# Turning rows into channel order: 32x32 blocks on VectorE and a trip through DRAM in place of TensorE transposes

## The chip, the cores and the metric

The kernel runs on one core of a Trainium2 chip. Its engines are TensorE (PE in the profile, its weight loads PEld), VectorE (DVE), ScalarE (ACT), GpSimd (POOL) and SyncE (SP); SyncE and GpSimd here mostly issue DMAs. The metric is the device time of one execution in microseconds, lower is better, given as the median of several runs.

## The reference

One decoder layer on x of 2048 tokens by 1024 channels, float32, batch 1:

```python
h = _rmsnorm(x, norm1_w)
proj = h @ w_in                                   # 1024 -> 3840 columns
hg_p, rw_p = proj[..., :HG_COLS], proj[..., HG_COLS:]
o_hg = _hgrn2_mixer(...)                          # 4 heads of 128, gated linear recurrence, chunks of 64
rw_p = rw_p + (_token_shift(rw_p) - rw_p) * rw_shift_mu
o_rw = _rwkv7_mixer(...)                          # 8 heads of 64, delta-rule state update
x = x + concatenate([o_hg, o_rw], axis=-1) @ w_out
x = x + _conv_ffn(_rmsnorm(x, norm2_w), w_up, conv_w, conv_b, w_down)
return _rmsnorm(x, final_norm_w)

def _rmsnorm(x, w):
    return x * rsqrt(mean(x * x, axis=-1) + 1e-6) * w
```

The norms need a token's whole row in one partition (tokens on partitions, channels along the free axis). The matrix products need the channels on partitions. So each normed block has to be transposed.

## The kernel before

The tokens are cut into NBLK = 4 blocks of BLK = 512. Phase 1 (up to some 1330 us) does the first norm, the input projection, both mixers and the output projection; phase 2 the up projection, the convolution and the down projection. Matrix products run in three terms (mm3: high by high, high by low, low by high), on operands split into two float32r parts.

Phase 1 is written as three streams that are interleaved by hand: dense (line 516), rw_stream (a super-step of two head pairs, rw_super, line 647) and hg_stream (one head, hg_unit, line 942). Each pass of the last loop takes one step of the two recurrent streams and then as much of the dense stream as a credit of TICK = 2000 ns pays for (fill, line 1100); the numbers that dense yields (648 for a projection's three matmuls, 436 for four transposes) are these costs. The framework's scheduler then makes each engine's order from this program; within an engine (and a DMA queue) instructions run strictly in that order.

The dense stream's jobs of a block are one "A" (the block's operand hh, hl gets ready), then 30 "P" (a projection of 128 columns, eight steps of three matmuls into a bank of the pair "pj", emptied by ScalarE and VectorE). From block 2 on, an "O" (the output projection of block nb - 2, out_block, line 379) stands ahead of "A". A list called extra puts further jobs between these, by position from "A":

- load4 (line 420) loads 512 rows into row_tile, the one tile "xt" of 128 x 4 x 1024, as four DMAs of 128 rows; norm4 (line 427) scales each row by its reciprocal root mean square (rstd, line 128, on ScalarE).
- For the next block's x: "E" load at +18, norm at +22, and "T" at +25, which is turn (line 437): for each of the KD = 8 slices of 128 channels, four TensorE transposes into a pj bank, which ScalarE copies back into xt in place. Later split_h (line 447), called during the last job before the next "A", multiplies by norm1_w (per partition) and splits into hh and hl.
- For the second norm of block nb - 2 (blocks 0 and 1): load at +6 of x1d (the sum of x and the output projection, in DRAM), norm at +10, and "N" at +11, which is transposed (line 258) with to_h2 (line 490): four transposes a slice into pj, ScalarE empties the bank with norm2_w as a scale per partition, and SyncE's queue stores the slice to h2d in DRAM, from which phase 2 reads.

The first block's x is transposed in another way, at the start, and blocks 2 and 3 of the second norm in phase 2; neither is touched.

Most DMAs go through SyncE's queue (the function dma). Two of its users matter for the chain: in rw_super, Ed<-M (line 745) stores parts of the masked products M to DRAM and E<-Ed (line 748) loads them back in the layout in which VectorE solves the triangular systems (lines 800 and 802). The ring "wraw" (four buffers of 2 KB per partition) holds raw weights in block 0, raw w_out tiles in "O", and the squares of rstd.

Of the kernel before, what the change touches and what calls it, by code (L numbers as in the profile page):

```python
# [7 lines left out]
F32 = mybir.dt.float32  # L8
# [4 lines left out]
ALU = mybir.AluOpType  # L13
# [54 lines left out]
def tile_layer(ctx, tc, consts, x, norm1_w, w_in, hg_lb_logits, hg_norm_w, rw_shift_mu, rw_w0, rw_w2,  # L68
# [14 lines left out]
    def row_tile():  # L83
        return xp_.tile([P, 4, D], F32, tag="xt", name="xt", bufs=1)
# [29 lines left out]
    def act(out_, in_, func, **kw):  # L114

        want = tables.get(func)
        if want is not None and want != tab["now"]:
            pre = S.preload_act_table_set(want)
            for u_ in tab["uses"]:
                tc.add_manual_dep(pre.ins, u_.ins.name, NOSYNC, reason="table order")  # L120
            tab.update(now=want, pre=pre, uses=[])
        i_ = S.activation(out_, in_, func, **kw)  # L122
        if want is not None:
            tc.add_manual_dep(i_.ins, tab["pre"].ins.name, NOSYNC, reason="table order")
            tab["uses"].append(i_)
        return i_

    def rstd(pool, xt, name, sqt="nsq", sqb=1):

        sq = pool.tile([P, D], BF16, tag=sqt, name="nsq", bufs=sqb)  # L130
        st = pool.tile([P, 2], F32, tag="nst", name=name, bufs=8)
        act(sq, xt, AF.Square, accum_out=st[:, 0:1])
        act(st[:, 1:2], st[:, 0:1], AF.Ln, bias=eps6, scale=1.0 / D)
        act(st[:, 1:2], st[:, 1:2], AF.Exp, scale=-0.5)
        return st[:, 1:2]
# [23 lines left out]
    def vec(nm, i):  # L159
        return vt[:, off[nm] + i:off[nm] + i + 1]  # L160
# [23 lines left out]
    oT = [dp.tile([D, BLK], F32, name=f"oT{b}") for b in range(NBLK)]  # L184
    x1d = [dp.tile([BLK, D], F32, name=f"x1d{b}") for b in range(NBLK)]
    h2d = [dp.tile([D, BLK], F32, name=f"h2d{b}") for b in range(NBLK)]
    gd_ = [dp.tile([FF, BLK], F32, name=f"gd{b}") for b in range(NBLK)]
    KH = NFF // 2
    DS = 5
# [84 lines left out]
    def phase1(c1):  # L274
# [22 lines left out]
        def bank(kind):  # L297
            return ps.tile([P, 512], F32, tag=kind, name=kind, bufs=2)
# [119 lines left out]
        rows = {}  # L418

        def load4(key, src, r0):  # L420
            def f():
                rows[key] = row_tile()
                for i in range(4):
                    dma(rows[key][:, i, :], src[r0 + i * P:r0 + (i + 1) * P, :])
            return f

        def norm4(key):
            def f():
                for i in range(4):
                    t_ = rows[key][:, i, :]  # L430
                    V.tensor_scalar_mul(t_, t_, rstd(wp, t_, "nst", "wraw", 4))
            return f

        def four_tiles(t_):
            return [t_[:, i, :] for i in range(4)]

        def turn(nb):

            t_ = rows[nb]
            for k in range(KD):  # L440
                tp = bank("pj")
                for i in range(4):
                    TE.transpose(tp[:, i * P:(i + 1) * P], t_[:, i, k * P:(k + 1) * P], ident)
                act(t_[:, :, k * P:(k + 1) * P], tp.rearrange("p (i t) -> p i t", i=4), AF.Copy)
                yield 436

        def split_h(nb, k):

            src, w = rows[nb][:, :, k * P:(k + 1) * P], vec("n1", k)
            h4, l4 = (t_[:, k, :].rearrange("p (i t) -> p i t", i=4) for t_ in (hh, hl))  # L450
            act(h4, src, AF.Copy, scale=w)
            V.scalar_tensor_tensor(l4, src, w, h4.bitcast(F32), ALU.mult, ALU.subtract)

        def next_block(nb, k):

# [30 lines left out]
        def to_h(k, tp, w):  # L486
            act(hh[:, k, :], tp, AF.Copy, scale=w)
            V.scalar_tensor_tensor(hl[:, k, :], tp, w, hh[:, k, :].bitcast(F32), ALU.mult, ALU.subtract)  # L488

        def to_h2(nb):  # L490
            def evict(k, tp, w):
                t_ = wp.tile([P, BLK], F32, tag="wraw", name="h2", bufs=4)
                act(t_, tp, AF.Copy, scale=w)
                dma(h2d[nb][k * P:(k + 1) * P, :], t_)
            return evict

        def constants():

# [17 lines left out]
        def dense():  # L516
# [27 lines left out]
            for nb in range(NBLK):  # L544
                if nb + 1 < NBLK:
                    extra += [(at[nb] + 18, ("E", load4(nb + 1, x[0], (nb + 1) * BLK))),
                              (at[nb] + 22, ("E", norm4(nb + 1))), (at[nb] + 25, ("T", nb + 1))]
                if nb >= 2:
                    extra += [(at[nb] + 6, ("E", load4(("N", nb - 2), x1d[nb - 2], 0))),
                              (at[nb] + 10, ("E", norm4(("N", nb - 2)))), (at[nb] + 11, ("N", nb - 2))]  # L550
            for m in range(2):
                extra += [(at[3] + 14 + 5 * m, ("E", sum_load(m))), (at[3] + 17 + 5 * m, ("E", sum_make(m)))]
            extra += [(at[3] + 25 + m, ("W", 2, o_take(m))) for m in range(4)]
# [27 lines left out]
            for n, jb in enumerate(jobs):  # L581
                if jb[0] == "E":
                    jb[1]()
                    continue
                if jb[0] == "A":
                    if jb[1] == 0:
                        banks = spread()
                        ahead = transposed(four_tiles(rows[0]), "n1", lambda: next(banks), to_h)
                    continue
                if jb[0] == "T":  # L590
                    yield from turn(jb[1])
                    continue
                if jb[0] == "N":
                    yield from transposed(four_tiles(rows.pop(jb)), "n2", lambda: bank("pj"), to_h2(jb[1]))
                    continue
                if jb[0] in "OW":
                    while done["rw2"] < 2 * jb[1] + 2 or done["hg"] < 4 * jb[1] + 4:
                        yield None
                    if jb[0] == "W":
                        jb[2]()  # L600
                    else:
                        yield from (out_block(2, *rows["O"]) if jb[1] == 2 else out_block(jb[1], then=jb[1] + 2))
                    continue
                _, col, ev, cond, fin = jb
                while not cond():
                    yield None
                load(i)
                ws = loaded.pop(i)
                if i == 0:
                    next(ahead)  # L610
                    next(ahead)
                    constants()
                load(i + 1)
                i += 1
                acc = bank("pj")
                then = jobs[n + 1][1] if jobs[n + 1][0] == "A" else None
                for k in range(KD):
                    wh, wl = ws[k // 4]
                    next(ahead, None)
                    mm3(acc, (wh[:, k % 4, :], wl[:, k % 4, :]), (hh[:, k, :], hl[:, k, :]), k == 0, k == KD - 1)  # L620
                    if k == KD - 1:
                        ev(acc)
                        if fin is not None:
                            fin()
                    next_block(then, k)
                    yield 648
# [996 lines left out]
```

## Time and profile before

| | us |
|---|---|
| median of 3 runs | 2657.88 |
| lowest and highest | 2653.09, 2657.88 |
| the profiled execution | 2662.58 |
| its span in the trace | 2660.8 |
| PE busy | 2560.2 (96%) |
| DVE busy | 1952.9 (73%) |
| ACT busy | 1389.2 (52%) |
| POOL busy | 380.4 (14%) |

Busy time is the union of an engine's instructions; a matmul's recorded duration overlaps the next one's, since matmuls are pipelined. A row of the groups reads: line, engine, operation, tile written <- tiles read, shapes, count | busy us, mean ns of one | idle us of the engine just before them, and what ended it. Lines are those of the kernel before; in the changed kernel the same code stands 1 to 10 lines lower. PEclk is the granted TensorE clock as a share of full speed.

### The profile page before, as it was taken

The numbers are of one execution on the slowest core, as the hardware profiler recorded it, in microseconds if no ns is written. First come the engines' busy times: TensorE is split into PE (matmuls) and PEld (weight loads), VectorE is DVE, ScalarE is ACT, GpSimd is POOL, SyncE is SP. The second block draws the span as 40 slices with busy tenths as digits, with TensorE's granted clock in tenths as the row PEclk, the third lists the DMA queues.
The fourth block names the chain that finished last, engine by engine and source line by source line (L and its number), as shares of the span: only waits on it lengthen the run. The fifth ranks groups of instructions, "written<-read, shape, count | busy, mean of one in ns | idle before, by whom it ended". The sixth has DMA issues, their size and how long they took to land. (4 is left out here: it accounts for less than half of the span.)

```text
span 2660.8 us, 51050 instructions
## 1 busy us (share of the span) xinstructions
PE 2560.2 (96%) x19595; PEld 2061.2 (77%) x19595; DVE 1952.9 (73%) x3728; ACT 1389.2 (52%) x2274; POOL 380.4 (14%) x686
## 2 busy tenths in 40 slices
PE   7999999989999999999899999999999999999998
PEld 5777777766777777777678888887888887888887
DVE  4877667576567765767678789987998887766556
ACT  5566453545535555445456754456545544545444
POOL 6433222212222122222100000000000000000000
PEclk9999999999999999999999999999999999999999
DMA  8645443445643456744493468646763553998665
GB/s 303 204 165 170 158 143 120 130 148 203 199 143 126 156 196 199 276 131 136 154 309 113 143 204 266 233 154 225 245 203 131 166 189 127 327 320 286 197 191 186
DMA packets 312714, 510.59 MB, mean 192 GB/s; under 512 B 46879, under 2 KB 143509, under 8 KB 312469
## 3 DMA queue, kind: packets, MB, share of 16 engines
q1 hardware_dynamic: 257937, 328.99, 37.4%
q0 software_dynamic: 54464, 178.32, 20.4%
q8 instruction: 154, 2.52, 0.4%
q14 instruction: 91, 0.75, 0.1%
q10 hardware_dynamic: 68, 0.02, 0.0%
HBM read 372.99 MB, written 134.22 MB: 191 GB/s over the span
## 5 line engine op out<-in xcount | busy, mean ns | idle before, releaser
L270 PE MATMUL pj<-hh,wh 128*128 128x512 f32 x960 | 393.4, 410 | 6.2 <-ACT rkv L122 3.3
L271 PE MATMUL pj<-hl,wh 128*128 128x512 f32 x960 | 377.8, 394 | 1.3 <-issue 1.3
L272 PE MATMUL pj<-hh,wl 128*128 128x512 f32 x960 | 377.5, 393 | 0.0
L270 PE MATMUL ua<-Bh,uwh 128*128 128x512 f32 x704 | 276.4, 393 | 4.4 <-ACT m L122 3.1
L272 PE MATMUL ua<-Bh,uwl 128*128 128x512 f32 x704 | 274.6, 390 | 0.0
L271 PE MATMUL ua<-Bl,uwh 128*128 128x512 f32 x704 | 274.3, 390 | 0.0
L270 PEld LDWEIGHTS pj<-hh,wh 128*128 128x128 f32 x960 | 181.5, 189 | 55.2 <-issue 8.7
L272 PEld LDWEIGHTS pj<-hh,wl 128*128 128x128 f32 x960 | 181.1, 189 | 40.6 <-issue 1.7
L271 PEld LDWEIGHTS pj<-hl,wh 128*128 128x128 f32 x960 | 181.6, 189 | 34.3 <-DVE hl L488 0.5
L254 ACT CAST uwh<-uraw 128x512 fp32r<-128x512 f32 x220 | 134.2, 617 | 128.9 <-PE ua L271 55.7
L255 DVE TENSOR_TENSOR dal<-draw,dah 128x512 fp32r<-128x512 f32 x138 | 95.4, 691 | 113.4 <-ACT dah L254 113.2
L255 DVE TENSOR_TENSOR uwl<-uraw,uwh 128x512 fp32r<-128x512 f32 x220 | 147.6, 688 | 34.9 <-ACT uwh L254 34.8
L254 ACT CAST dah<-draw 128x512 fp32r<-128x512 f32 x138 | 85.7, 621 | 164.9 <-PE da L271 80.6
L270 PEld LDWEIGHTS ua<-Bh,uwh 128*128 128x128 f32 x704 | 132.2, 188 | 34.1 <-ACT m L122 5.7
L272 PEld LDWEIGHTS ua<-Bh,uwl 128*128 128x128 f32 x704 | 132.3, 188 | 28.1 <-DVE uwl L255 0.4
L271 PEld LDWEIGHTS ua<-Bl,uwh 128*128 128x128 f32 x704 | 132.3, 188 | 26.7
L270 PE MATMUL ud<-Bh,uwh 128*128 128x512 f32 x352 | 138.1, 392 | 0.0
L272 PE MATMUL ud<-Bh,uwl 128*128 128x512 f32 x352 | 137.2, 390 | 0.0
L271 PE MATMUL ud<-Bl,uwh 128*128 128x512 f32 x352 | 137.1, 390 | 0.0
L1493 POOL DMA_DIRECT2D gd<-y x2 | 1.1, 540 | 946.8 <-DVE y L1491 946.8
L271 PE MATMUL da<-dbl,dah 128*128 128x512 f32 x332 | 129.5, 390 | 0.2 <-DVE dbl L255 0.2
L272 PE MATMUL da<-dbh,dal 128*128 128x512 f32 x332 | 129.3, 389 | 0.0
(584 smaller groups left out, 6233.9 us busy)
## 6 DMA issues: line engine op xcount, KB each, us to landing
uraw<-in_w_up_dram SPq DMA_DIRECT2D x176, 256.0 KB, 3.1
woraw<-in_w_out_dram POOLq DMA_DIRECT2D x96, 256.0 KB, 3.6
br<-gd SPq DMA_DIRECT2D x88, 256.0 KB, 4.2
draw<-Sg SPq DMA_DIRECT2D x88, 256.0 KB, 3.3
draw<-Tw SPq DMA_DIRECT2D x88, 256.0 KB, 4.0
gd<-y SPq DMA_DIRECT2D x86, 256.0 KB, 2.9
Sg<-br SPq DMA_DIRECT2D x72, 256.0 KB, 2.1
xt<-x1d SPq DMA_DIRECT2D x32, 512.0 KB, 6.7
```

The lines of the kernel that those rows point to most:

```text
L254: S.copy(hi, src)
L255: V.tensor_sub(lo, src, hi.bitcast(F32))
L270: TE.matmul(acc, lh, rh, start=first, stop=False, skip_group_check=skip)
L271: TE.matmul(acc, lh, rl, start=False, stop=False, skip_group_check=skip)
L272: TE.matmul(acc, ll, rh, start=False, stop=last, skip_group_check=skip)
L1493: (dma if end is None else nc.gpsimd.dma_start)(gd_[2 * h + b][fb * P:(fb + 1) * P, :], ys[0][:, b * BLK:(b + 1) * BLK])
```

## The change

For the x rows of blocks 1, 2 and 3 and the second norm of blocks 0 and 1, the TensorE transposes go. load4 now puts the 512 rows into xt so that partition group g (32 partitions) holds the 128 tokens g * 128 to g * 128 + 127, as four runs i of 32. turn becomes one VectorE transpose in 32x32 blocks for each slice of 128 channels, from xt into a tile "turned" of the ring wraw, and four stores (one for each partition group, 32 partitions x 4 runs of 512 bytes) that put the blocks in channel order into a DRAM tile: the new hT for x, h2d for the second norm. For x a new function back loads hT into a new xt, eight DMAs of 128 x 512, and split_h reads that. For the second norm the weight norm2_w is broadcast to all partitions (two tiles n2row) and multiplied in norm4, along with the row's scale.

The jobs "T" and "N" go. The eight turns of x stand at +23 to +26, two at each position, and back at +29; of the second norm, the norm stands at +9 and its turns at +10 to +13. The yields of 436 go with the transposes, so the dense stream's other jobs move up against the two recurrent streams, and the scheduler makes all orders anew.

```diff
--- before.py
+++ after.py
@@ -184,6 +184,7 @@
     oT = [dp.tile([D, BLK], F32, name=f"oT{b}") for b in range(NBLK)]
     x1d = [dp.tile([BLK, D], F32, name=f"x1d{b}") for b in range(NBLK)]
     h2d = [dp.tile([D, BLK], F32, name=f"h2d{b}") for b in range(NBLK)]
+    hT = [dp.tile([D, BLK], F32, name=f"hT{b}") for b in range(NBLK)]
     gd_ = [dp.tile([FF, BLK], F32, name=f"gd{b}") for b in range(NBLK)]
     KH = NFF // 2
     DS = 5
@@ -418,38 +419,58 @@
         rows = {}
 
         def load4(key, src, r0):
+
             def f():
                 rows[key] = row_tile()
-                for i in range(4):
-                    dma(rows[key][:, i, :], src[r0 + i * P:r0 + (i + 1) * P, :])
+                v = src[r0:r0 + BLK, :].rearrange("(g i t) d -> g t i d", g=4, i=4)
+                for g in range(4):
+                    dma(rows[key][g * 32:g * 32 + 32], v[g])
             return f
 
         def norm4(key):
             def f():
+                w = None
+                if isinstance(key, tuple):
+                    w = [wp.tile([P, BLK], F32, tag="wraw", name="n2row", bufs=4) for _ in range(2)]
+                    for c in range(2):
+                        dma(w[c], norm2_w[0:1, c * BLK:(c + 1) * BLK].broadcast_to([P, BLK]))
                 for i in range(4):
                     t_ = rows[key][:, i, :]
-                    V.tensor_scalar_mul(t_, t_, rstd(wp, t_, "nst", "wraw", 4))
+                    r_ = rstd(wp, t_, "nst", "wraw", 4)
+                    if w is None:
+                        V.tensor_scalar_mul(t_, t_, r_)
+                        continue
+                    for c in range(2):
+                        h_ = t_[:, c * BLK:(c + 1) * BLK]
+                        V.scalar_tensor_tensor(h_, h_, r_, w[c], ALU.mult, ALU.mult)
             return f
 
         def four_tiles(t_):
             return [t_[:, i, :] for i in range(4)]
 
-        def turn(nb):
-
-            t_ = rows[nb]
-            for k in range(KD):
-                tp = bank("pj")
-                for i in range(4):
-                    TE.transpose(tp[:, i * P:(i + 1) * P], t_[:, i, k * P:(k + 1) * P], ident)
-                act(t_[:, :, k * P:(k + 1) * P], tp.rearrange("p (i t) -> p i t", i=4), AF.Copy)
-                yield 436
+        def turn(key, dst, k):
+
+            def f():
+                y = wp.tile([P, 4, 4, 32], F32, tag="wraw", name="turned", bufs=4)
+                V.transpose(y.rearrange("p c i t -> p i c t"),
+                            rows[key][:, :, k * P:(k + 1) * P].rearrange("p i (c t) -> p i c t", t=32))
+                for g in range(4):
+                    dma(dst[k * P:(k + 1) * P, g * P:(g + 1) * P].rearrange("(c p) x -> p c x", p=32),
+                        y[g * 32:g * 32 + 32].rearrange("p c i t -> p c (i t)"))
+            return f
+
+        def back(nb):
+            def f():
+                t_ = rows[nb] = row_tile().rearrange("p i (a t) -> p (i a) t", t=BLK)
+                for k in range(KD):
+                    dma(t_[:, k, :], hT[nb][k * P:(k + 1) * P, :])
+            return f
 
         def split_h(nb, k):
 
-            src, w = rows[nb][:, :, k * P:(k + 1) * P], vec("n1", k)
-            h4, l4 = (t_[:, k, :].rearrange("p (i t) -> p i t", i=4) for t_ in (hh, hl))
-            act(h4, src, AF.Copy, scale=w)
-            V.scalar_tensor_tensor(l4, src, w, h4.bitcast(F32), ALU.mult, ALU.subtract)
+            src, w = rows[nb][:, k, :], vec("n1", k)
+            act(hh[:, k, :], src, AF.Copy, scale=w)
+            V.scalar_tensor_tensor(hl[:, k, :], src, w, hh[:, k, :].bitcast(F32), ALU.mult, ALU.subtract)
 
         def next_block(nb, k):
 
@@ -486,13 +507,6 @@
         def to_h(k, tp, w):
             act(hh[:, k, :], tp, AF.Copy, scale=w)
             V.scalar_tensor_tensor(hl[:, k, :], tp, w, hh[:, k, :].bitcast(F32), ALU.mult, ALU.subtract)
-
-        def to_h2(nb):
-            def evict(k, tp, w):
-                t_ = wp.tile([P, BLK], F32, tag="wraw", name="h2", bufs=4)
-                act(t_, tp, AF.Copy, scale=w)
-                dma(h2d[nb][k * P:(k + 1) * P, :], t_)
-            return evict
 
         def constants():
 
@@ -544,10 +558,12 @@
             for nb in range(NBLK):
                 if nb + 1 < NBLK:
                     extra += [(at[nb] + 18, ("E", load4(nb + 1, x[0], (nb + 1) * BLK))),
-                              (at[nb] + 22, ("E", norm4(nb + 1))), (at[nb] + 25, ("T", nb + 1))]
+                              (at[nb] + 22, ("E", norm4(nb + 1))), (at[nb] + 29, ("E", back(nb + 1)))]
+                    extra += [(at[nb] + 23 + k // 2, ("E", turn(nb + 1, hT[nb + 1], k))) for k in range(KD)]
                 if nb >= 2:
                     extra += [(at[nb] + 6, ("E", load4(("N", nb - 2), x1d[nb - 2], 0))),
-                              (at[nb] + 10, ("E", norm4(("N", nb - 2)))), (at[nb] + 11, ("N", nb - 2))]
+                              (at[nb] + 9, ("E", norm4(("N", nb - 2))))]
+                    extra += [(at[nb] + 10 + k // 2, ("E", turn(("N", nb - 2), h2d[nb - 2], k))) for k in range(KD)]
             for m in range(2):
                 extra += [(at[3] + 14 + 5 * m, ("E", sum_load(m))), (at[3] + 17 + 5 * m, ("E", sum_make(m)))]
             extra += [(at[3] + 25 + m, ("W", 2, o_take(m))) for m in range(4)]
@@ -586,12 +602,6 @@
                     if jb[1] == 0:
                         banks = spread()
                         ahead = transposed(four_tiles(rows[0]), "n1", lambda: next(banks), to_h)
-                    continue
-                if jb[0] == "T":
-                    yield from turn(jb[1])
-                    continue
-                if jb[0] == "N":
-                    yield from transposed(four_tiles(rows.pop(jb)), "n2", lambda: bank("pj"), to_h2(jb[1]))
                     continue
                 if jb[0] in "OW":
                     while done["rw2"] < 2 * jb[1] + 2 or done["hg"] < 4 * jb[1] + 4:
```

## The prediction

> **What bounds the kernel now.** The page's first part comes first: busy time, share of the span and instructions of each engine.
>
> ```profile
> span 2660.8 us, 51050 instructions
> PE 2560.2 (96%) x19595; PEld 2061.2 (77%) x19595; DVE 1952.9 (73%) x3728; ACT 1389.2 (52%) x2274; POOL 380.4 (14%) x686
> ```
>
> TensorE (PE) is busy for 96% of the span and VectorE (DVE) for 73%, but those are averages over two phases. The second view cuts the span where phase 1 gives way to the up projection; the change touches phase 1 alone. The third is the same view for the five stretches in which rows are now transposed (the order is x rows for block 1, for block 2, x1 rows of block 0, x rows for block 3, x1 rows of block 1).
>
> ```profile
> core 0: us, PE busy (x) PEld busy (x) DVE busy (x) ACT busy (x) POOL busy (x), PEclk, DMA share, GB/s
> 60.00:1330.00 1270.00, 1203.42 (x13618) 946.24 (x13617) 870.90 (x2072) 651.69 (x1078) 327.93 (x592) 0.99 0.51 167
> ...
> 180.00:220.00 40.00, 36.91 (x292) 28.09 (x292) 33.06 (x59) 33.91 (x51) 14.65 (x24) 0.98 0.51 174
> 480.00:520.00 40.00, 36.92 (x207) 27.57 (x206) 31.63 (x46) 26.55 (x36) 7.46 (x14) 0.96 0.36 112
> 680.00:720.00 40.00, 38.95 (x228) 30.28 (x227) 30.59 (x47) 27.68 (x42) 12.34 (x22) 1.00 0.59 191
> 820.00:860.00 40.00, 38.05 (x220) 28.89 (x220) 32.51 (x51) 27.04 (x38) 8.53 (x16) 1.00 0.37 120
> 1020.00:1060.00 40.00, 38.95 (x229) 30.35 (x228) 29.99 (x47) 27.22 (x41) 10.23 (x18) 1.00 0.55 177
> sum 200.00, PE 189.79 PEld 145.19 DVE 157.78 ACT 142.41 POOL 53.21; mean PE 37.96 PEld 29.04 DVE 31.56 ACT 28.48 POOL 10.64
> ```
>
> In phase 1 TensorE is idle for 1270 - 1203.4 = 66.6 us only: its queue is nearly always full, so time taken off TensorE should come off the span unless something else starts to be late. In the five stretches it is idle for 10.2 us of 200, and VectorE for 42.2 us of 200. That 42.2 us is the room into which the change puts its new work. DMA is busy for half of its time or less and is not a bound by volume.
>
> **What TensorE gives back.** Three turns of x and two of the second norm go: 5 x 32 = 160 transposes of 128x128. Their price is not their duration. The timeline of the first turn shows the pitch.
>
> ```profile
> 214.83 0.39 PE L271 MATMUL pj<-hl,wh 128*128 128x512 f32 x1
> 215.06 0.39 PE L272 MATMUL pj<-hh,wl 128*128 128x512 f32 x1
> 215.29 0.60 PE L443 MATMUL pj<-ident,xt 128*128 128x128 f32 x4
> 217.88 0.70 PE L443 MATMUL pj<-ident,xt 128*128 128x128 f32 x4 [1.99 <-ACT hf L122]
> 219.41 2.43 PE L443 MATMUL pj<-ident,xt 128*128 128x128 f32 x10
> ```
>
> The next view has the groups of instructions, costliest first, for 60 to 1400 us (busy, mean ns of one, idle time of the engine before them); these rows also carry the prices used further down.
>
> ```profile
> L313 DVE SCALAR_TENSOR_TENSOR rkv<-pj,vt,rkv 128x511 f32<-128x511 f32 x43 | 32.1, 747 | 60.0 <-ACT rkv L122 59.8
> L812 DVE STREAM_TRANSPOSE TTs<-TZ 32x512 f32<-32x512 f32 x32 | 22.5, 703 | 0.8
> L443 PE MATMUL pj<-ident,xt 128*128 128x128 f32 x96 | 16.1, 313 | 4.9 <-ACT hf L122 4.1 <-ACT xt L122 0.8
> L431 DVE TENSOR_SCALAR xt<-xt,nst 128x1024 f32<-128x1024 f32 x20 | 14.1, 753 | 0.4 <-ACT nst L122 0.4
> L122 ACT ACTIVATE xt<-pj 128x512 f32<-128x512 f32 x24 | 13.7, 598 | 3.7 <-PE pj L443 3.6
> L122 ACT ACTIVATE h<-pj,vt 128x512 f32<-128x512 f32 x16 | 10.3, 684 | 8.2 <-PE pj L264 7.8 <-ACT h L122 0.4
> L264 PE MATMUL pj<-ident,xt 128*128 128x128 f32 x64 | 9.9, 284 | 0.8 <-ACT hv L122 0.5
> L806 DVE STREAM_TRANSPOSE TZ<-Ti 128x512 f32<-128x512 f32 x8 | 8.4, 1055 | 0.2
> ```
>
> Four transposes end 0.60 us after the first began, though one lasts some 0.27 us by itself: the pitch is (0.60 - 0.27) / 3 = 0.11 us, and the lower bound of the gain is 160 x 0.11 = 17.6 us. But the ten at 219.41 run at about (2.43 - 0.27) / 9 = 0.24 us each, just after a wait of 1.99 us for ScalarE to empty a PSUM bank of the pair pj. The groups' busy time holds such stretches: 16.1 + 9.9 = 26.0 us, and the waits before them 4.9 + 0.8 = 5.7 us, so the upper bound is 31.7 us. The waits come of the turn's use of pj (two banks, shared with the projections), and they go with it; whether the slow pitch goes wholly is open, so I take the middle: -24.7 us.
>
> [...]
>
> The order of TensorE's queue at the first turn (part is the split operand of a head-group norm in the RWKV chain), before:
>
> ```order
> L272 MATMUL pj<-hh,wl 128x512
> L443 MATMUL pj<-ident,xt 128x128 x8
> L1081 MATMUL rw<-part,group 128x512
> L443 MATMUL pj<-ident,xt 128x128 x10
> L1082 MATMUL rw<-part,group 128x512
> L1081 MATMUL rw<-part,group 128x512
> L1082 MATMUL rw<-part,group 128x512
> L443 MATMUL pj<-ident,xt 128x128 x14
> L270 MATMUL pj<-hh,wh 128x512
> ```
>
> and of the changed kernel at the same place (its lines are numbered 1 or 10 higher):
>
> ```order
> L272 MATMUL pj<-hl,wh 128x512
> L1091 MATMUL rw<-part,group 128x512
> L273 MATMUL pj<-hh,wl 128x512
> L271 MATMUL pj<-hh,wh 128x512
> ...
> L273 MATMUL pj<-hh,wl 128x512
> L1092 MATMUL rw<-part,group 128x512
> L1091 MATMUL rw<-part,group 128x512
> L1092 MATMUL rw<-part,group 128x512
> ```
>
> Nothing takes the place of the 32 transposes: the projection's matmuls close up, and ten of them now stand between the chain's first matmul and its second.
>
> **What VectorE takes on.** Forty transposes of 128x512 in 32x32 blocks (8 for each turn). Two rows bound one: 0.70 us (L812) and 1.06 us (L806). L806 reads with a stride of 16 elements; the new ones read and write runs of 32 elements, which is nearer to L812. I take 0.70: 40 x 0.70 = 28.1 us; the other end is 42.2 us. The second norm's weight, which ScalarE applied while it emptied PSUM (h, 684 ns), moves into the row scaling: per row tile, one 753 ns operation becomes two of about 747 ns (L313, the same form), so 8 x (2 x 0.747 - 0.753) = +5.9 us. Together +34.0 us, at most +48.1. ScalarE loses 13.7 + 10.3 = 24.0 us of evictions; I count no gain for that beyond the waits above. split_h reads the same 512 elements, now contiguous: the same price.
>
> VectorE's queue at the first turn of the second norm, before (M are the masked products that the triangular solve waits for):
>
> ```order
> L713 SCALAR_TENSOR_TENSOR AR<-mk,W 128x2x512
> L431 TENSOR_SCALAR xt<-xt,nst 128x1024 x4
> L718 TENSOR_TENSOR KB<-mk,ai 128x8x128
> ...
> L733 TENSOR_TENSOR M<-rw,cst 128x2x2x128 x2
> ```
>
> and after (KB's last writer is L728, M's L743):
>
> ```order
> L445 SCALAR_TENSOR_TENSOR xt<-xt,nst,n2row 128x512 x8
> L249 TENSOR_TENSOR part<-BV,part 128x1024
> ...
> L455 STREAM_TRANSPOSE turned<-xt 128x4x4x32 x2
> L723 SCALAR_TENSOR_TENSOR AR<-mk,W 128x2x512
> ...
> L728 TENSOR_TENSOR KB<-mk,ai 128x8x128
> L455 STREAM_TRANSPOSE turned<-xt 128x4x4x32 x2
> L371 SCALAR_TENSOR_TENSOR hgg<-pj,vt,sgm 128x512
> L455 STREAM_TRANSPOSE turned<-xt 128x4x4x32
> L743 TENSOR_TENSOR M<-rw,cst 128x2x2x128 x2
> ```
>
> About 6.0 us of scaling and 3.5 us of transposes now stand ahead of M where 3.0 us stood. The idle 42.2 us of the five stretches would hold 34.0 us only if it lay in the right places, so some of the added time delays the RWKV chain, and TensorE waits where its queue has nothing else ahead. The bounds are none of it (TensorE has the projections as filler) and all of it. The stretches are 79% full of VectorE already and would be 96% full; I charge three tenths, nearer to none because TensorE's present waits on VectorE are small. The largest in 66 to 1320 us (who waited for whom: total, times, longest):
>
> ```profile
> PE hg L1063 <- DVE SH L1055: 5.1, 3, 4.1
> PE hg L1042 <- DVE hk L1035: 5.0, 5, 1.6
> PE rw L819 <- DVE TZ L806: 2.3, 3, 1.0
> ```
>
> So +0.3 x 34.0 = +10.2 us.
>
> **What the queues take on.** SyncE's queue gets 160 stores of 64 KB in place of 16 of 256 KB, 24 loads to bring x back, and 4 broadcasts of the norm weight. Its present rows: issue (minimum, median, maximum ns) of the norm's store, of Ed<-M (32 partitions, 64 KB, nearest to the new stores) and its landing, and the timeline around the first turn, of SyncE and of the instructions that it serves.
>
> ```profile
> L494 SPq DMA_DIRECT2D h2d<-h x16: 319/320/941, 711.7 to 1058.2; - x16
> L745 SPq DMA_DIRECT2D Ed<-M x32: 318/500/1177, 95.8 to 1205.8; - x32
> DMA to landing us min/median/max: 2.0/3.3/4.7
> ...
> 205.51 0.34 SPq L1076 DMA_DIRECT2D oT<-osq  x1
> 237.78 1.95 SPq L745 DMA_DIRECT2D Ed<-M  x4
> 244.30 1.10 SPq L748 DMA_DIRECT2D E<-Ed  x2
> 279.50 1.78 SPq L424 DMA_DIRECT2D xt<-in_x_dram  x4
> ...
> 229.91 1.28 DVE L733 TENSOR_TENSOR M<-rw,cst 128x512 f32<-128x512 f32 x2
> ...
> 235.27 2.48 DVE L733 TENSOR_TENSOR M<-rw,cst 128x512 f32<-128x512 f32 x4 [1.34 <-PE rw L730]
> ...
> 265.60 0.72 ACT L122 ACTIVATE hh<-xt,vt 128x512 fp32r<-128x512 f32 x1
> ```
>
> 172 more issues at 0.32 to 0.50 us are 55 to 86 us of a queue that does nothing for 30 us at a time; four issues for a transposed tile (2.0 us) fit behind the next. The loads of x and x1 keep their number and size. Its order at the first turn, before:
>
> ```order
> L1076 DMA oT_143<-osq 128x512
> L937 DMA oT_143<-yo 128x2x512
> L1076 DMA oT_143<-osq 128x512
> L745 DMA Ed<-M 32x16x32 x4
> L748 DMA E<-Ed 64x1024 x2
> ```
>
> after:
>
> ```order
> L1086 DMA oT_143<-osq 128x512
> L458 DMA hT_156<-turned 32x4x128 x20
> L947 DMA oT_143<-yo 128x2x512
> L1086 DMA oT_143<-osq 128x512
> L458 DMA hT_156<-turned 32x4x128 x12
> L466 DMA xt<-hT_156 128x512 x5
> L755 DMA Ed<-M 32x16x32 x4
> L466 DMA xt<-hT_156 128x512 x3
> L758 DMA E<-Ed 64x1024 x2
> ```
>
> The loads of xt wait until the stores of hT have landed, and Ed<-M, the triangular solve's input, is queued behind five of them. The last two transposes stand ahead of M in VectorE's queue, so their stores (2.0 us of issue, 3.3 us to land) and five loads (2.5 us) end 8 us behind them, while M itself took from 229.9 to 237.7 us. I cost this at nothing; the cover is M's own time, and without it the solve starts up to 5 us late. The loaded rows are first read by split_h at 265.6 us, 28 us later, and in the blocks that follow an output projection stands between, so that reading is not late. GpSimd's queue keeps its order; its weight loads in block 0 share the four wraw buffers with the transposed tiles, which costs prefetch depth for four projection columns, covered by a column's 24 matmuls (5.4 us at 0.227 us).
>
> **The sum.** -24.7 + 10.2 = -14.5 us. The profiled execution took 2662.6 us (span 2660.8), 0.18% above the median of 2657.9, so I put the change on the median: 2643.4, say 2643 us. A difference within 0.2% (5.3 us) is about what a measurement of this kernel cannot tell from none.
>
> **The rivals.**
> 1. *VectorE is fully hidden* and all of 31.7 us comes off: 2626 us. For it: ScalarE, 34 of 40 us busy at 180 to 220, is relieved exactly there. Against: VectorE's queue above.
> 2. *VectorE becomes the bound in the turns.* Its place is the chain from the scaling to M, where the five stretches fill up; its price is the whole added time, 2658 - 17.6 + 34.0 = 2674 us (2689 with the long transposes). It turns the sign once 52 to 73% of the added 34 us reaches TensorE (17.6 / 34.0, 24.7 / 34.0). Against: phase 1's TensorE waits on VectorE are a few us each. [...]
> 3. *SyncE's queue holds back the solve*: Ed<-M and E<-Ed late behind hT and h2d stores, about 5 us in each of five turns, 25 us against the 24.7 gained: 2658 us. For it: VectorE's solve already waits for E.
>
> ```profile
> DVE etmp L800 <- DMA E<-Ed: 19.8, 5, 5.7
> ```
>
> Against: TensorE has the projections as filler there.
>
> **How the numbers follow.** Forecast 0.54 (its own range 2632 to 2652); all hidden 0.15; VectorE bound 0.18; queue 0.13. Faster: the first two and a little of the third queue case, 0.70; within 0.2%: most of the queue case, 0.13; slower: VectorE bound less its mild end, 0.17. The range 2626 to 2664 leaves out part of the first rival below and most of the second above.
>
> **What would show it.** Right: no transposes into pj, TensorE's busy time in phase 1 down by 18 to 26 us, the new transposes near 0.70 us, VectorE's turn stretches close to full, TensorE's waits on VectorE up by about 10 us. Wrong: transposes of 1 us or more, or E<-Ed or hh named in waits of several us by TensorE. The queues' new order everywhere (the schedule is made anew) may shift a few us that no step here accounts for.

## The result, and the profile after

| | before | after |
|---|---|---|
| median (6 runs each) | 2657.88 us | 2668.07 us |
| lowest and highest | 2653.09 to 2667.32 | 2664.35 to 2672.49 |
| ratio, 95% interval | 1 | 1.0032 [1.0019, 1.0045] |
| span of the profiled execution | 2660.8 us | 2666.2 us |

The change made the kernel slower by 0.32%, some 8.5 us, where the prediction had 14.5 us faster. (A ratio, here and below, is the recorded one with its interval; it is not the quotient of the two medians.) The page after, its first part:

```profile
span 2666.2 us, 50995 instructions
PE 2549.7 (96%) x19435; PEld 2048.2 (77%) x19435; DVE 1979.8 (74%) x3776; ACT 1363.0 (51%) x2230; POOL 381.3 (14%) x686
```

TensorE has its 160 transposes less, and is busy for 10.5 us less. The groups that VectorE took on:

```profile
L455 DVE STREAM_TRANSPOSE turned<-xt 128x512 f32<-128x512 f32 x40 | 27.1, 693 | 1.8 <-DMA hT<-turned 1.7
L445 DVE SCALAR_TENSOR_TENSOR xt<-xt,nst,n2row 128x512 f32<-128x512 f32 x16 | 10.8, 744 | 0.0
```

Both are as priced (0.70 and 0.747 us). So VectorE's instructions cost what was foreseen and yet the span grew. The same windows of phase 1 as before, and a stretch of it around the output projection of block 1; first after:

```profile
60.00:1330.00 1270.00, 1187.42 (x13447) 929.90 (x13446) 893.34 (x2113) 623.81 (x1031) 327.29 (x590) 0.98 0.58 178
880.00:1010.00 130.00, 113.26 (x1176) 84.66 (x1175) 79.43 (x183) 59.23 (x103) 25.57 (x48) 0.93 0.58 169
```

and the second of them before:

```profile
880.00:1010.00 130.00, 120.70 (x1434) 92.15 (x1433) 89.54 (x214) 64.74 (x115) 29.10 (x55) 1.00 0.56 186
```

TensorE's idle time in the 1270 us rose from 66.6 to 82.6 us. In the 130 us it rose from 9.3 to 16.7 us, and there the granted clock (the column behind POOL) fell from 1.00 to 0.93. From 60 us to the first matmul of the up projection TensorE is idle for 84.0 us after and loses 27.3 us to a lower clock (from the trace's clock records); before, it is 68.6 and 17.1. That is 26 us more lost, while the work itself got 21 us shorter. TensorE's largest waits after (60 to 1400 us; "issue" is time in which the engine waited for nothing that the profile shows) and two of its waits for weights:

```profile
PE pj L271 <- ACT hh L248: 12.1, 10, 2.0
PE hg L998 <- issue: 11.6, 8, 2.3
PE pj L271 <- ACT wh L255: 3.1, 2, 2.5
PE pj L271 <- DMA wh<-Win171h: 2.2, 1, 2.2
```

Before, the first two stood at

```profile
PE pj L270 <- ACT hh L247: 6.4, 7, 1.4
PE hg L988 <- issue: 2.4, 2, 2.1
```

and no wait on a DMA for a weight tile (Win) stood in its list. Sorted by what ended them, TensorE's waits on VectorE did not grow (the rows add up to 29.0 us before and 28.5 after); those on ScalarE did by 4 us, those named issue by 7 us, those on a DMA from none to 6.7 us. The rows named issue, ACT wh and DMA come back below.

### The profile page after: what moved, and what is told of

It reads as the page before. It is cut to its first block, busy times and chain, and to the rows that moved or that the text cites. A ratio compares the mean times of both kernels' runs of the same rounds, so it can differ in the third digit from the quotient of the medians.

```text
span 2666.2 us, 50995 instructions
## 1 busy us (share of the span) xinstructions
PE 2549.7 (96%) x19435; PEld 2048.2 (77%) x19435; DVE 1979.8 (74%) x3776; ACT 1363.0 (51%) x2230; POOL 381.3 (14%) x686
## 4 chain that ended last, share of the span: by engine, by line
PE 62%; issue 13%; DMA 8%; DVE 8%; ACT 5%; POOL 3%; SPq 0%; POOLq 0%; DVEq 0%; ACTq 0%
PE ua L271 5%; PE ua L273 5%; PE ua L272 5%; PE pj L271 5%; PE pj L272 4%; PE pj L273 4%; PE ud L272 3%; PE ud L271 3%; PE ud L273 3%; PE da L272 3%; PE da L273 3%; PE da L271 3%; PE db L273 2%; PE db L272 2%; PE db L271 2%
```

## The experiments

Four theories. D: the row loads, now four transfers of 32 partitions instead of 128, land late and hold up the weight loads queued beside them. V: VectorE's added time delays the RWKV chain. W: the broadcasts of norm2_w do it, through the ring wraw. O: the order does it; with the yields of 436 gone, 40 x 436 ns = 17.4 us of dense work stand earlier against the two recurrent streams, in order and not in time. Each new kernel was run 4 to 10 times. Each set of runs has its own 19 to 29 runs of the kernel before, so ratios are compared. Over the sets its median lay between 2655.92 and 2660.26 us.

**The two halves and the loads.** load32 is the kernel before with only the loads changed (and the order in which ScalarE writes what it takes out of PSUM, so that the tokens come out right):

```diff
-                for i in range(4):
-                    dma(rows[key][:, i, :], src[r0 + i * P:r0 + (i + 1) * P, :])
+                v = src[r0:r0 + BLK, :].rearrange("(g i t) d -> g t i d", g=4, i=4)
+                for g in range(4):
+                    dma(rows[key][g * 32:g * 32 + 32], v[g])
```

> The kernel before, with one part of the change alone: the rows of x and of x1 are loaded as in the changed kernel, four DMAs of 32 partitions x 4 rows instead of four of 128 partitions; TensorE transposes as before and ScalarE's eviction puts the tokens in order (an access pattern, the same elements). Theory D (the row loads on 32 partitions hold up the other DMAs, above all the weight loads, and TensorE waits for weights): slower than before by 3 to 10 us, row loads land in 10 to 14 us instead of 6 to 9, weight loads behind them in 9 to 12 us instead of 6 to 7, TensorE waits named by DMA wh or wl of some 4 to 7 us. Theory V (VectorE's added 34 us) and theory O (the order made anew): no change beyond 0.2%, 2653 to 2663 us.

load16 is the changed kernel with those loads cut:

```diff
-                for g in range(4):
-                    dma(rows[key][g * 32:g * 32 + 32], v[g])
+                for i in range(4):
+                    for g in range(4):
+                        t0 = r0 + g * P + i * 32
+                        dma(rows[key][g * 32:g * 32 + 32, i, :], src[t0:t0 + 32, :])
```

> The changed kernel, with each row load of 32 partitions x 4 rows cut into four of 32 partitions x 1 row, issued so that neighbours in the queue write different partition groups (16 issues a block instead of 4, the same packets). Theory D, if it is the concentration on 32 partitions at a time: weight loads behind them land in 6 to 8 us again, TensorE's waits for wh and wl (6.5 us in the changed kernel) go, and the time falls by 4 to 10 us to 2658 to 2664. If the 4 KB packets are slow for another reason, or under V and O: no change, 2663 to 2672.

x_only keeps the change for x and puts the second norm back on TensorE, with its old loads and ScalarE's weight; n2_only does it the other way round (only the job lists are shown):

```diff
x_only:  -  ("E", turn(("N", nb - 2), h2d[nb - 2], k))     +  ("N", nb - 2)
n2_only: -  ("E", turn(nb + 1, hT[nb + 1], k))             +  ("T", nb + 1)
```

> Half of the change: the x rows of blocks 1 to 3 are turned by VectorE and through DRAM, the second norm stays on TensorE with 128-partition loads and ScalarE's weight. VectorE gains 24 x 0.69 = 16.6 us, TensorE loses 96 transposes (10.6 us at pitch, up to 21 with their waits). Theory V or the second norm's broadcasts (n2row, the ring wraw) as the cause: faster than the changed kernel by 8 us or more, 2645 to 2658. Theory D: the x loads at 720 us still hold up weights, the x1 loads at 635 and 980 us no longer: 2655 to 2663. Theory O: anything within 8 us of either kernel.

> The other half: the second norm of blocks 0 and 1 by VectorE, x by TensorE with 128-partition loads. VectorE gains 16 x 0.69 + 5.9 = 16.9 us, TensorE loses 64 transposes (7 us at pitch). If the loss of the changed kernel sits in the second norm (its largest new losses are at 950 to 1000 and 1050 to 1100 us): slower than before by 5 to 10 us, 2663 to 2668. If it is spread by VectorE's time: within 3 us of the middle, 2660 to 2665. Theory D: weight waits at 635 to 660 and 980 to 1000 us, none at 720 to 740.

| | median us | ratio to before |
|---|---|---|
| load32 | 2664.59 | 1.0017 [1.0002, 1.0031] |
| load16 | 2660.31 | 0.9996 [0.9986, 1.0006] |
| x_only | 2652.94 | 0.9968 [0.9956, 0.9980] |
| n2_only | 2664.88 | 1.0019 [1.0006, 1.0032] |

D holds in both directions: the new loads alone slow the kernel before by 0.17% (the interval only just leaves out no difference), and cutting them takes 0.36% (9.6 us) off the change. The time from issue to landing of a row load, before, after, load32, load16:

```profile
DMA to landing us min/median/max: 6.2/7.7/9.1
```

```profile
DMA to landing us min/median/max: 5.4/12.3/14.5
```

```profile
DMA to landing us min/median/max: 5.6/8.7/11.7
```

```profile
DMA to landing us min/median/max: 3.6/6.0/7.5
```

A weight tile that is loaded just behind the x1 rows, around 986 us (kind, queue, count, KB, median us to landing), before and after:

```profile
wl<-Win171l POOLq DMA_DIRECT2D x1, 256.0 KB, 7.3
```

```profile
wl<-Win171l POOLq DMA_DIRECT2D x1, 256.0 KB, 12.4
```

In load32 TensorE's waits for weights add up to 5.8 us (before: none), though the row loads themselves landed in 8.7 us, less than the 10 to 14 us expected. So late weights go with these loads in both kernels, and the 12.3 us of after are not the work of 32 partitions alone; what else made them longer is not shown.

But cut loads only bring the change back to no difference: the 21 us by which TensorE's work got shorter are still missing from the gain. Of the halves, x gains 0.32% and the second norm loses 0.19%; together they would gain 0.13%, and the whole change loses 0.32%, so the halves are not independent.

**VectorE, the broadcasts, the order.** All on cut loads. x_only16 has them in x_only. twice16 makes each transpose twice:

```diff
                 V.transpose(y.rearrange("p c i t -> p i c t"), ...)
+                V.transpose(y.rearrange("p c i t -> p i c t"), ...)
```

no_n2w16 makes norm4 take its path without a weight (it leaves norm2_w out for blocks 0 and 1), paced16 gives the count back (the edits are shortened):

```diff
no_n2w16: -  if isinstance(key, tuple):          +  if False:
paced16:  -  ("E", turn(...))                    +  ("Y", turn(...))
          +  if jb[0] == "Y":
          +      jb[1]()
          +      yield 436
          +      continue
```

> Only x is turned by VectorE (the second norm stays on TensorE, as before the change), and each row load of x is cut into four of 32 partitions x 1 row (16 issues instead of 4). Theory D (row loads confined to 32 partitions hold up the weight loads behind them): x has three of the five row loads that cost the whole change 8 to 9 us, so three fifths of that, some 5 us, come off the 2652.9 us of the same kernel with whole loads: 2648 us, ratio about 0.9955. Rival (the loads of x fall where no weight is awaited, and only those of x1 cost anything): 2652 to 2654 us, ratio 0.997 to 0.998.

> The changed kernel with cut row loads (2660.3 us), and each of the 40 VectorE transposes made twice into the same tile: 40 x 0.69 = 27.7 us more of VectorE, nothing else. Theory V (VectorE's added time delays the RWKV chain, and this is what keeps the change from paying): at three tenths, as the prediction charged, +8 us, 2668 us; at half, +14 us, 2674 us. Rival (VectorE's added time is hidden, the loss is in loads and in the order of TensorE's queue): 0 to +3 us, 2660 to 2663 us.

> The changed kernel with cut row loads (2660.3 us), without the second norm's weight for blocks 0 and 1: it leaves out the four broadcasts of norm2_w (256 KB each, into the ring wraw) and scales a row tile by one instruction instead of two (8 x 0.735 = 5.9 us less VectorE). Theory V alone (three tenths of VectorE's time): -2 us, 2658 us. Theory W (the broadcasts and their buffers in the ring hold up the weight tiles or the row tiles behind them): -4 to -8 us, 2652 to 2656 us. If the second norm's loss is neither: 2660 us, as it was.

> The changed kernel with cut row loads (2660.3 us); each turn job now counts for the order as the four TensorE transposes did that it replaced (436 each), so that the order of the dense work against the RWKV chain goes back towards that of before. Theory O (what is lost is the order: without that count the dense work runs some 18 us ahead of the chain and then waits for it): the waits go and some 5 to 9 us with them, 2651 to 2655 us. Rivals D, V and W (loads, VectorE, broadcasts): the order is beside the point, 2658 to 2662 us.

| | median us | ratio to before |
|---|---|---|
| x_only16 | 2649.50 | 0.9972 [0.9961, 0.9982] |
| twice16 | 2655.07 | 0.9996 [0.9983, 1.0009] |
| no_n2w16 | 2663.81 | 1.0026 [1.0011, 1.0042] |
| paced16 | 2643.16 | 0.9942 [0.9920, 0.9963] |

V falls: 27.7 us more of VectorE changed nothing. W finds no support: without the broadcasts and with 5.9 us less of VectorE the kernel is slower by 0.3%, not faster. But the order moved with it, so the run gives no price for the broadcasts by themselves. One wait, not there in load16, shows how a smaller job moves the rest:

```profile
PE rw L830 <- DVE lastc L316: 7.5, 1, 7.5
```

What shifted it stays open. x_only16 gave the rival's number: cutting the loads of x in x_only brings nothing. x_only has no wait for a weight tile in its list and n2_only has 6.5 us of them, so in the two halves D's cost lies with the x1 loads. And O is worth 0.54% (load16 against paced16), with all instructions and loads as they were.

**The order by itself, and what it hides.** paced is paced16 with whole loads, paced16x2 has 872 in place of 436, paced16_twice makes each transpose twice. unpaced is the kernel before with the counts of its transposes at nothing:

```diff
unpaced: -                yield 436
         +                yield 0
         -            yield 109 * n
         +            yield 0 if xt[0].shape[0] == P and nm == "n2" else 109 * n
```

> The changed kernel with its own whole row loads, and only the count given back: each turn job counts 436 for the order, as the four transposes did. Theory O (the order is most of the loss) with D (whole loads of 32 partitions cost some 4 to 9 us in any order): ratio to before 0.9942 + 0.0017 to 0.0034 = 0.996 to 0.9976. Rival (in the good order the late weights have cover, so the loads cost nothing): 0.994 to 0.995. Rival to O (paced16 gained by something that only cut loads allow): 1.000 or more.

> The kernel before with all its TensorE transposes, but those of the five turns no longer counted for the order (their 436 and 109 x 4 become 0): nothing is removed, moved to another engine or loaded in another form, the dense work just stands some 17 us earlier against the RWKV chain. Theory O (dense work ahead of the chain is what costs): +5 to +14 us, ratio 1.002 to 1.005. Rival (the order alone is beside the point): within 0.999 to 1.001.

> As paced16 (ratio 0.9942), with 872 instead of 436 for each turn job: the dense work falls back some 17 us behind where it stood before. If it is the lead of the dense work over the chain that costs (theory O) and more lag goes on helping: 0.990 to 0.993. If the place that it had before was the tuned one, off it on either side it costs: 0.996 to 1.000. If the count does nothing: 0.994.

> As paced16 (ratio 0.9942), each of the 40 VectorE transposes made twice: +27.7 us of VectorE. Theory V (it was hidden in twice16 only because that kernel waited elsewhere; in the better order VectorE's time shows): three tenths, +8 us, 0.997. Rival (VectorE's added time is hidden at these places): 0.994 to 0.9955.

| | median us | ratio to before |
|---|---|---|
| paced | 2654.26 | 0.9982 [0.9971, 0.9992] |
| unpaced | 2676.00 | 1.0062 [1.0040, 1.0084] |
| paced16x2 | 2657.96 | 0.9992 [0.9982, 1.0002] |
| paced16_twice | 2648.48 | 0.9954 [0.9938, 0.9969] |

unpaced settles that the order alone can cost this much: nothing is removed from the kernel before or moved off an engine, and it is slower by 0.62%, no less than the change and more than was expected. It has the same two waits as the changed kernel in the output projection (wh are weights that ScalarE rounds, xh is the sum by which VectorE empties the banks). The timeline of after (start us, us, engine, line, operation, out<-in, idle before and its releaser):

```profile
973.77 0.73 PE L271 MATMUL pj<-wh,hh 128*128 128x512 f32 x2 [2.52 <-ACT wh L255]
978.71 0.80 PE L271 MATMUL pj<-hh,wh 128*128 128x512 f32 x1 [2.49 <-DVE xh L414]
```

of unpaced:

```profile
990.08 0.73 PE L270 MATMUL pj<-wh,hh 128*128 128x512 f32 x2 [2.50 <-ACT wh L254]
995.02 0.50 PE L270 MATMUL pj<-hh,wh 128*128 128x512 f32 x1 [2.52 <-DVE xh L413]
```

and of before, where both are short:

```profile
979.98 0.73 PE L270 MATMUL pj<-wh,hh 128*128 128x512 f32 x2 [0.22 <-ACT wh L254]
985.74 0.50 PE L270 MATMUL pj<-hh,wh 128*128 128x512 f32 x1 [0.50 <-DVE xh L413]
```

The pair (2.5 us, then 1.8 to 2.5) stands in after, load16, twice16, no_n2w16 and unpaced, in every kernel that has the full lead, and in no other kernel of this study. The largest row that the count removes is another one, TensorE's waits named issue in hg. They add up to 11.6 us in after and 12.5 in load16; with the count, in paced, the row reads

```profile
PE hg L1002 <- issue: 2.6, 3, 1.2
```

In unpaced they are 4.5 us, so the two kernels do not lose their time in all the same places. The windows 880 to 1010 us of unpaced, then of paced16:

```profile
880.00:1010.00 130.00, 112.79 (x1256) 85.14 (x1257) 86.96 (x211) 64.01 (x113) 24.80 (x46) 0.95 0.49 162
```

```profile
880.00:1010.00 130.00, 120.14 (x1225) 90.68 (x1226) 76.27 (x161) 63.85 (x108) 32.07 (x60) 1.00 0.63 194
```

With the count, busy time (120.1 of 130 us) and clock (1.00) are those of before again. The first matmul of the up projection, the end of what the change touches, in before, after, unpaced and paced16:

```profile
1373.77 0.39 PE L270 MATMUL ua<-Bh,uwh 128*128 128x512 f32 x1
```

```profile
1378.18 0.39 PE L271 MATMUL ua<-Bh,uwh 128*128 128x512 f32 x1
```

```profile
1387.08 0.39 PE L270 MATMUL ua<-Bh,uwh 128*128 128x512 f32 x1
```

```profile
1352.92 0.39 PE L271 MATMUL ua<-Bh,uwh 128*128 128x512 f32 x1
```

The loads still cost 0.40% in the good order (paced against paced16, from two sets; the two intervals leave some 0.16 to 0.64%), a little more than the forecast for paced allowed. In paced, TensorE waits for weights as in after; first its waits on a DMA, then those of paced16:

```profile
PE pj L273 <- DMA wl<-Win170l: 3.5, 2, 1.9
PE pj L271 <- DMA wh<-Win170h: 2.9, 2, 2.2
PE pj L273 <- DMA wl<-Win131l: 1.8, 1, 1.8
PE pj L273 <- DMA wl<-Win171l: 1.5, 1, 1.5
```

```profile
PE pj L273 <- DMA wl<-Win200l: 2.5, 2, 1.9
PE pj L273 <- DMA wl<-Win201l: 1.2, 2, 0.7
PE pj L271 <- DMA wh<-Win200h: 0.2, 1, 0.2
```

Twice the count loses it again (0.9992). paced16_twice shows VectorE's price in a kernel that waits less: 27.7 us more cost 0.12%, 3.2 us, about a tenth; the intervals overlap, and by themselves they leave room for anything from nothing to 0.39%.

**Lead or place, the best kernel, and a control.** tick16 takes the lead away evenly (load16, TICK from 2000 to 1950); pace_x16 and pace_n16 count only the turns of x or only those of the second norm; x_only16_paced counts x's turns in x_only16. before_x2 and before_tick are the kernel before with only the order moved: 872 in place of 436 in x's turns, and TICK 1950.

```diff
tick16, before_tick: -TICK = 2000.0          +TICK = 1950.0
pace_x16:            -("Y", turn(("N", ...   +("E", turn(("N", ...
pace_n16:            -("Y", turn(nb + 1, ... +("E", turn(nb + 1, ...
x_only16_paced:      -("E", turn(nb + 1, ... +("Y", turn(nb + 1, ...
before_x2:           -yield 436              +yield 872
```

> The changed kernel with cut row loads and no counts at the turns (ratio 0.9996); instead the credit that a step of the two recurrent streams gives the dense stream falls from 2000 to 1950 ns, which takes the lead away evenly over phase 1. Theory O as a lead (what counts is how far dense work stands ahead of the chain): most of the 0.54% comes, ratio 0.994 to 0.9965. Theory O as a place (what counts is where the count falls, next to the turns): 0.998 to 1.002.

> The changed kernel with cut row loads (0.9996), with the count of 436 only for the 24 turns of x. Lead: three fifths of 0.54%, ratio 0.9964. Place at x: 0.994 to 0.995. Place at the second norm: 0.999 to 1.000.

> The changed kernel with cut row loads (0.9996), with the count of 436 only for the 16 turns of the second norm. Lead: two fifths of 0.54%, ratio 0.9974. Place at the second norm: 0.994 to 0.995. Place at x: 0.999 to 1.000.

> Only x by VectorE with cut loads (ratio 0.9972), with the count of 436 for its turns; the second norm on TensorE, which counts as before. If the order had cost the x half its share too (three fifths of 0.54%): 0.994, as much as paced16, and the second norm's half is then worth nothing. If the x half loses nothing by the order: 0.997, and the second norm's half is worth 0.3% (8 us) in a good order.

> The kernel before, with 872 instead of 436 for each of the 24 steps of x's turns: only the order moves, the dense work 10.5 us later against the RWKV chain. If the order of before is tuned: 1.000 to 1.005. If it is not, and dense work later at x's turns helps by itself (then the 0.9929 of the best kernel is partly that): 0.995 to 0.999.

> The kernel before, with a credit of 1950 instead of 2000 ns for a step: only the order moves, the dense work drifts later, by some 17 us over phase 1. If the order of before is tuned: 1.000 to 1.005. If dense work later helps by itself: 0.995 to 0.999.

| | median us | ratio to before |
|---|---|---|
| tick16 | 2656.34 | 0.9996 [0.9979, 1.0013] |
| pace_x16 | 2643.88 | 0.9946 [0.9927, 0.9965] |
| pace_n16 | 2652.14 | 0.9979 [0.9964, 0.9993] |
| x_only16_paced | 2637.34 | 0.9929 [0.9904, 0.9954] |
| before_x2 | 2665.86 | 1.0019 [1.0004, 1.0034] |
| before_tick | 2656.09 | 0.9992 [0.9980, 1.0003] |

It is the place, mainly at x's turns: the count there brings nearly all, the count at the second norm's turns a part (that both are worth less together than summed is plain: 0.50 + 0.17 against 0.54), and a lead taken away evenly brings nothing. This rests on tick16, and on paced16x2, which loses the gain with more lag; the lead's forecasts for the two halves (0.9964 and 0.9974) still lie inside the intervals of pace_x16 and pace_n16. tick16 has no such pair of waits and gains nothing, so the pair marks the bad order but is not the whole of its cost. What tick16 keeps is the wait named issue:

```profile
PE hg L999 <- issue: 12.5, 7, 3.0
```

It stands at 10.7 to 13.6 us in the five changed kernels without any count at the turns (after, load16, twice16, no_n2w16, tick16) and at 5.4 or less in all others. What it waits for stays open, and so does what else is in the cost. The control says that the order of before stands near an optimum in the count at x's turns (872 costs 0.19%); a smaller credit is worth nothing that shows (0.9992, with 1 inside the interval). So the kernels with counts do not owe their gain to an order that the kernel before lacked, as far as these two steps tell.

The best kernel is x_only16_paced, 0.71% faster than before. That it is at least as fast as paced16 (intervals overlap) means that the second norm's half of the change is worth nothing that shows, even in a good order. Its phase 1:

```profile
60.00:1330.00 1270.00, 1207.91 (x13608) 947.54 (x13607) 892.58 (x2114) 650.97 (x1072) 328.25 (x592) 0.99 0.57 182
```

TensorE is idle for 62.1 us there, less than before the change (66.6).

## Why the prediction was wrong

**The step that failed first** is "Nothing takes the place of the 32 transposes: the projection's matmuls close up". It read the changed order and priced it at nothing. The order is made from the counts, so taking 436 away at each turn moved all dense work behind it. Alone this costs 0.62% in the kernel before (unpaced), and 0.50% (13 us) in the changed one (after against paced). In the trace of after it shows as waits named issue and as the pair in the output projection; which wait makes which part of the 13 us stays open. The ten matmuls that now stood between the chain's steps were in the quoted rows; no term of the sum was made of them. The prediction's last sentence left a few us for the new order; it was 13.

**The second** is "The loads of x and x1 keep their number and size". They do, but each now goes to 32 partitions. Measured: 0.36% (load16 against after, 9.6 us), 0.40% in the good order, 0.17% in the kernel before (load32). The landing rows agree in direction (7.7 to 12.3 us in after, to 8.7 in load32). Why such a load takes longer is not shown; no run here separates the partitions that a load reaches from the cut's smaller size and other order of transfers.

**VectorE's three tenths** were too much by what was seen: 27.7 us more cost 0.0% (twice16) and 0.12% (paced16_twice), where three tenths would be 8.3 us or 0.31%. twice16 against load16 leaves room for some 0.16% and so excludes three tenths; paced16_twice by itself does not. What they test is a second 27.7 us beside the first, but TensorE's waits on VectorE did not rise in after either (29.0 to 28.5 us, where some 10 us more were expected). The prices of the instructions were right. Rival 2 (VectorE as the bound) is refuted by both runs that made the transposes twice; rival 1's mechanism, VectorE hidden, was nearly true, and not its time.

**SyncE's queue at nothing** held as far as the solve goes. The chain's wait that rival 3 feared became shorter; VectorE's row before and after:

```profile
DVE etmp L800 <- DMA E<-Ed: 19.8, 5, 5.7
```

```profile
DVE etmp L810 <- DMA E<-Ed: 5.1, 3, 4.5
```

**TensorE's 24.7 us** was right in size: the work from 60 us to the up projection, without waits and lower clock, got 21 us shorter in the trace. One reading in it was wrong. The slow pitch of the ten transposes at 219.41 (0.24 us against 0.11) was read as coming with the wait for PSUM; nearly all of them ran while the clock was at half, as the windows view of before shows (the column behind POOL, 0.50):

```profile
218.40:221.70 3.30, 3.06 (x14) 2.44 (x13) 3.30 (x5) 2.80 (x6) 1.83 (x3) 0.50 0.48 150
```

**The sum.** With the count kept and the loads cut (paced16) the change is worth 0.58%, 15.4 us [10, 21]; the prediction's -14.5 us is inside. Then 0.40% goes to the loads (paced) and 0.50% to the order (after): -0.58 + 0.40 + 0.50 = +0.32%. That this adds up is no test, since each term is the difference of two neighbouring kernels; but the other way round (loads first, 0.36, then the order, 0.54) gives nearly the same two sizes. So the two terms that were not costed had the larger sum. That the costed ones came so near is partly luck: with the price of VectorE's time that was seen, none to about a tenth, the same sum would have been -21 to -25 us, at or beyond the end of the interval. What takes the rest in paced16 is not shown.

## What to carry to other kernels

Where numbers in the code set the order of the streams, a change that takes work out also takes its number out: ask what that does to the order, and keep the number once as a control before judging the change. A transfer that keeps its bytes and its count but goes to fewer partitions is another transfer (512 KB of rows landed in 7.7 us before, in 8.7 in load32 and in 12.3 in after); look at how long it takes to land and who loads behind it. Run the order alone (the old work, the new counts) as one experiment: it showed in one run what no view of the profile had separated.

## What the runs showed of the hardware

Row loads of 512 KB to 32 partitions took 12.3 us to land where those to 128 took 7.7, and 256 KB weight loads beside them up to 12.4 where they had taken 7.3. In load32 the same 512 KB loads landed in 8.7 us, and TensorE waited for weights for 5.8 us. Cut into 128 KB pieces that go round the partition groups (load16), the row loads landed in 6.0 us. (Landing times of rows are medians.)

Half the clock followed a wait of TensorE of some 2 us at two places here (0.51 in after, 0.50 in before). Around the pair of waits the windows of after read:

```profile
973.00:976.00 3.00, 1.74 (x6) 0.97 (x6) 2.89 (x4) 1.94 (x5) 0.00 (x0) 1.00 0.44 161
976.00:983.00 7.00, 4.51 (x11) 3.39 (x11) 3.26 (x6) 0.71 (x1) 1.07 (x2) 0.51 0.78 214
```

The first wait ended at 973.8 us; the clock is 1.00 up to 976 us and 0.51 for the next 7 us, and the second wait (976.2 to 978.7) lies inside that slow stretch. So the second did not start it. In the kernel before, half clock at 218.4 us followed a single wait of 1.99 us that ended at 217.9. At these two places the longest wait was 2.52 and 1.99 us; what makes the clock fall is not shown. Idle time alone does not set the loss. Phase 1 of no_n2w16, then of paced:

```profile
60.00:1330.00 1270.00, 1190.83 (x13445) 933.67 (x13443) 886.04 (x2105) 623.88 (x1031) 327.56 (x590) 0.97 0.57 176
```

```profile
60.00:1330.00 1270.00, 1190.25 (x13486) 933.22 (x13485) 899.36 (x2126) 635.31 (x1046) 327.82 (x593) 0.99 0.58 180
```

TensorE is idle for 79.2 us in the first and for 79.8 in the second, and the granted clock is 0.97 and 0.99.
